# A head of column operations: part of one chunk's modulation on TensorE, its column operations moved, one weight load queued later

## The chip, the cores and the metric

The kernel runs on one core of a Trainium2 chip. The metric is device time in microseconds of one execution; the time shown for a kernel is the median of several executions. One further execution is recorded by the hardware profiler, and its trace is what is read below. TensorE (PE, with its weight loads PEld), VectorE (DVE), ScalarE (ACT), GpSimd (POOL) and SyncE (SP, which starts the DMAs) each run their own instructions in order and wait for one another by semaphores.

## The reference, cut to what matters

One layer of a decoder for 1024 tokens of width 1024: a mixing sub-layer (pooling and dilated window attention) and a gated MLP with a convolution, each between norms that are modulated by a conditioning vector. The change lies in the first lines, before the first projection:

```python
c_act = jax.nn.silu(c)
for l in range(DEPTH):
    mod = c_act @ w_ada[l] + b_ada[l]
    sh_m, sc_m, gt_m, sh_f, sc_f, gt_f = (t[:, None, :] for t in jnp.split(mod, N_MOD, axis=-1))
    h = rms_norm(x, g_pre_mix[l]) * (1.0 + sc_m) + sh_m
    y = mixing_sublayer(h, cos, sin, w_in[l], w_pool[l], b_pool[l], pool_scale[l], w_out[l])
    x = x + gt_m * rms_norm(y, g_post_mix[l])
    ...
```

`sh_m` and `sc_m`, 1024 numbers each, are what the touched code computes; `h @ w_in` inside `mixing_sublayer` is the projection that follows.

## The kernel before, in words

The head of the kernel works on six of the eight token tiles (`NS`) and goes through the width 1024 in eight chunks of 128 (`kc` from 0 to 7). For each chunk, `wa[kc]` holds the modulation weights: 128 partitions by eight pieces (`kb`) of 256 columns, 128 for the shift and 128 for the scale. The product with the conditioning vector goes in three steps. `mods_first` (L336 on ScalarE, L338 on VectorE) multiplies the pieces 0 and 1 by their column of `cact` into the two halves of `acc`. `mods(kc, 0)` adds the pieces 2 and 3, `mods(kc, 1)` the pieces 4 to 7 (six multiply-adds, L344) and then the two halves (L347), all on VectorE. `colsum` (L352) sums over the 128 partitions on TensorE: two matmuls of one column, with `acc` as the stationary operand, into the columns 256 and 257 of PSUM bank 7. `columns` (L355, L357, VectorE) makes of them one column of scale, `acol`, and one of shift, `bcol`.

Beside it, `turn` (L361) transposes the chunk of the six normalised token tiles into bank 6 and the first 256 columns of bank 7, and `h_chunk` lets ScalarE read them, apply `acol` and `bcol` and write `h` (L419) and its rounded copy `hh` (L417 for chunk 0, a copy at L124 for the others). `low` (L425, VectorE) makes the rest `hl`. `proj` then multiplies by the weights, which `piece` and `lower` (L391) have split into `wh` and `wl` in the same way: `hh` by `wh` and by `wl` (L410, L411), `hl` by `wh` (L407), into banks 0 to 5, one per token tile.

The order of all this is written out by hand for TensorE, ScalarE, VectorE and GpSimd. In the round of chunk `kc`, TensorE transposes chunk `kc`, sums its columns and projects chunk `kc - 1`, while VectorE adds up chunk `kc + 1`. Ahead of the rounds, three groups of `WARM` matmuls (L366, five each) on a constant stand between the norms of the token tiles. A weight chunk's buffer is one of three; chunk 4 takes that of chunk 1.

Behind the head, only TensorE's order is written by hand; a queue `Q` counts a slot for every group of three projection matmuls and runs tasks at their slot. The other engines' order is set by a scheduler. There, `unit_piece(1, j)` loads and splits a piece of the next unit's weights.

Of the kernel before, what the change touches and what calls it, by code (L numbers as in the profile page):

```python
# [12 lines left out]
AF = mybir.ActivationFunctionType  # L13
ALU = mybir.AluOpType

P = 128
# [63 lines left out]
WARM = (5, 5, 5)  # L80
NB = 2
# [24 lines left out]
def block_kernel(ctx: ExitStack, tc: tile.TileContext, x, pos, cols, rows, consts, w_ada_a, w_ada_b, w_in_u,  # L106
# [119 lines left out]
    NS = 6  # L226
# [65 lines left out]
    with tc.tile_pool(name="st", bufs=2) as st:  # L292
# [37 lines left out]
        def mods_first(kc, eng):  # L330
            if kc >= NK:
                return
            accs[kc] = st.tile([P, 2, 256], F32, name="acc", tag="acc", bufs=2)
            for i in range(2):
                if eng is nc.scalar:
                    nc.scalar.activation(accs[kc][:, i], wa[kc][:, i], AF.Copy, scale=cact[:, i:i + 1])  # L336
                else:
                    nc.vector.tensor_scalar_mul(accs[kc][:, i], wa[kc][:, i], cact[:, i:i + 1])  # L338

        def mods(kc, part):  # L340
            if kc >= NK:
                return
            for kb in range(4, 8) if part else (2, 3):
                nc.vector.scalar_tensor_tensor(accs[kc][:, kb % 2], wa[kc][:, kb], cact[:, kb:kb + 1],  # L344
                                               accs[kc][:, kb % 2], op0=ALU.mult, op1=ALU.add)
            if part:
                nc.vector.tensor_add(accs[kc][:, 0], accs[kc][:, 0], accs[kc][:, 1])  # L347

        def colsum(kc):
            for i in range(2):  # L350
                o, c = PS[:, 7, 256 + i:257 + i], slice(i * P, (i + 1) * P)
                nc.tensor.matmul(o, accs[kc][:, 0, c], ones[:, 0:1], start=True, stop=True)  # L352

        def columns(kc):
            nc.vector.tensor_scalar(acol[:, kc:kc + 1], PS[:, 7, 257:258], bsc1[:, kc:kc + 1], cl("g_pre_mix", kc),  # L355
# [3 lines left out]
        def turn(kc, ts_):  # L359
            for t in ts_:  # L360
                nc.tensor.transpose(PS[:, 6 + t // 4, (t % 4) * P:(t % 4 + 1) * P], xt[t][:, kc * P:(kc + 1) * P],  # L361
                                    ident)

        def warm(n):
            for _ in range(n):
                nc.tensor.matmul(bank(5, P), ones, ones, start=True, stop=True)  # L366
# [23 lines left out]
        def lower(j, wh, wl):  # L390
            nc.vector.tensor_tensor(wl, raws[j], wh.bitcast(F32), ALU.subtract)  # L391
# [35 lines left out]
        with tc.manual_schedule(engines={ET.PE, ET.Activation, ET.DVE, ET.Pool}):  # L427
            order = START.split()
            at = [0]

            def loads(n):
                for _ in range(n):
                    if at[0] < len(order):
                        load(order[at[0]][0], int(order[at[0]][1]))
                        at[0] += 1

            loads(FIRST_LOADS)
            nc.scalar.activation(cact, cl("c"), AF.Silu)
            angles()
            root(epst)  # L440
            mods_first(0, nc.vector)
            for part in range(2):
                mods(0, part)
            for t in range(0, NS, NB):
                norm_a(t, NB)
                if t == 0:
                    colsum(0)
                if t == NS - NB:
                    wh, wl = piece(0, False)
                norm_b(t, NB)  # L450
                turn(0, range(t, t + NB))
                warm(WARM[t // 2])
                if t == 0:
                    columns(0)
            h32 = h_chunk(0)
            mods_first(1, nc.vector)
            lower(0, wh, wl)
            mods(1, 0)
            mods(1, 1)
            low(0, h32)  # L460
            for kc in range(1, NK):
                loads(LOADS[kc])
                if kc == 1:
                    proj(0, 0, range(SPL))
                turn(kc, range(NS))
                if kc == 1:
                    proj(0, 0, range(SPL, NS))
                colsum(kc)
                mods_first(kc + 1, nc.scalar)
                mods(kc + 1, 0)  # L470
                columns(kc)
                h32 = h_chunk(kc)
                if kc == NRM:
                    norm_b(NS, 2)
                if kc in SQ_AT:
                    squares(NS + SQ_AT.index(kc))
                if kc == SQ_AT[1]:
                    roots[NS] = root(ssq[:, NS:NS + 2], 2)
                if kc > 1:
                    proj(kc - 1, 0)  # L480
                mods(kc + 1, 1)
                low(kc, h32)
                if kc in (1, 3, 5):
                    piece((kc + 1) // 2)
                proj(kc - 1, 1)
                if kc == 7:
                    turn_rest(0)
            loads(len(order))
            rest = h_rest(0)
            l_rest(0, rest)  # L490
            for t in range(NS):
                if t == RT:
                    turn_rest(1)
                proj(7, 0, (t,))
                proj(7, 1, (t,))
                if t < 2:
                    evac(un, t, t)
            piece(4)
            rope(un, 0)
            h32 = h_rest(1)  # L500
            l_rest(1, h32)
            piece(5)
            nc.vector.tensor_copy(cact2, cact)
# [96 lines left out]
    with tc.tile_pool(name="bp", bufs=1) as bp, tc.manual_schedule(engines={ET.PE}):  # L600
# [216 lines left out]
        for ui in range(5):  # L817
            if ui:
                un = Unit(ui, ws)
            un.V = new_v()  # L820
            if prev is not None:
                attend(prev, Q.slot + LAG_S)
            if ui == 1:
                catB = r2.tile([P, 2, 2, S], F32R, name="catB", tag="r2c")
                cat[2:4] = [(catB[:, 0, c], catB[:, 1, c]) for c in range(2)]
            if ui == 4:
                wps = [load_piece(w_in_p[1], 1024)]
            if ui:
                nxt = []
                for j, at_ in enumerate(PIECES):  # L830
                    Q.after(at_, lambda j=j, nxt=nxt, u=ui + 1: nxt.append(unit_piece(u, j)))
            else:
                nxt = more_w + [unit_piece(1, j) for j in (2, 3)]
            if MU <= ui <= MU + 2:
                for hf in range(2):
                    due = Q.slot + MLAG[hf]
                    later = lambda f, ahead=False, due=due: Q.at(due - MSPL * ahead, f)
                    if ui > MU:
                        mod_col(ui - MU, 7, hf, fin_shift if ui == MU + 1 else fin_scale, later)
                    elif hf:  # L840
                        Q.after(MLAG[0] + 1, lambda later=later: mod_row(0, 2, 6, gtg, 7, 1, later))
                    else:
                        mod_row(0, 2, 6, gtg, 7, 0, later)
            project(un, prev)
            ws, prev = nxt, un
# [671 lines left out]
```

## Time and profile before

| | us |
|---|---|
| median of 3 runs | 1058.23 (1057.42 to 1058.69) |
| the profiled execution's own time | 1057.68 |
| its span, first to last instruction | 1055.9 |
| TensorE busy | 1029.5 |
| VectorE busy | 850.7 |
| ScalarE busy | 487.9 |

The span is cut into groups of instructions with start, duration and what they waited for. A start in a row is in microseconds from the first instruction; the brackets at the end of a row of the timeline give the idle time ahead of it and what ended it.

### The profile page before, as it was taken

What the parts mean: (1) busy time and instruction counts of PE and PEld (TensorE: products, weight loads), DVE (VectorE), ACT (ScalarE), POOL (GpSimd) and SP (SyncE); (2) the same over time, 40 slices, a digit from 0 to 9 for tenths busy, and PEclk for the clock granted to TensorE, in tenths of its full rate; (3) what the DMA queues carried; (4) which work ended last, traced back from release to release, by engine and by line L of the source; (5) the groups of instructions that cost most, each with busy time, mean ns of one, the idle gap of its engine ahead of it and who ended that gap; (6) DMA issues with size and microseconds to landing.
All of it is one profiled execution on the core that took longest, in us unless ns stands there. A gap on an engine that the chain in (4) does not pass through costs nothing.

```text
span 1055.9 us, 15450 instructions
## 1 busy us (share of the span) xinstructions
PE 1029.5 (97%) x5174; PEld 871.8 (83%) x5174; DVE 850.7 (81%) x1839; ACT 487.9 (46%) x964; POOL 217.3 (21%) x132
## 2 busy tenths in 40 slices
PE   4999999999999999999999999999999999999997
PEld 4988989889888777878888888888888888888885
DVE  7975467885458768999999898998998798756997
ACT  6765343433354369733433333333334365544642
POOL 0000000000000000244334233333342415103560
PEclk9999999999999999999999999999999999999999
DMA  9552436362132173225334344444553889567553
GB/s 362 220 158 88 115 113 215 82 183 78 51 96 52 31 259 134 105 81 189 124 125 168 117 139 145 165 153 142 175 190 104 306 278 344 157 192 229 185 204 120
DMA packets 85148, 168.34 MB, mean 159 GB/s; under 512 B 9158, under 2 KB 25926, under 8 KB 81356
## 3 DMA queue, kind: packets, MB, share of 16 engines
q1 hardware_dynamic: 85068, 167.35, 47.7%
q8 instruction: 41, 0.67, 0.3%
q14 instruction: 39, 0.32, 0.1%
HBM read 134.47 MB, written 32.84 MB: 158 GB/s over the span
## 4 chain that ended last, share of the span: by engine, by line
PE 89%; DVE 5%; DMA 2%; ACT 2%; issue 1%; SPq 0%; DVEq 0%; ACTq 0%
PE PS L1092 36%; PE PS L1397 20%; PE PS L222 6%; PE PS L224 5%; PE PS L223 5%; PE PS L714 3%; PE PS L684 2%; PE PS L704 1%; DVE acc L344 1%; PE PS L596 1%; PE PS L598 1%; PE PS L597 1%; DMA wa<-in_w_ada_a_dram 1%; PE PS L622 1%; PE PS L781 1%
## 5 line engine op out<-in xcount | busy, mean ns | idle before, releaser
L1165 POOL TENSOR_TENSOR raws<-rw 128x512 f32<-128x512 f32 x28 | 45.6, 1627 | 510.8 <-PE PS L1092 442.9
L222 PE MATMUL PS<-wh,hh 128*128 128x384 f32 x336 | 124.4, 370 | 0.1
L224 PE MATMUL PS<-wh,hl 128*128 128x384 f32 x336 | 113.2, 337 | 0.0
L223 PE MATMUL PS<-wl,hh 128*128 128x384 f32 x336 | 112.9, 336 | 0.0
L1397 PE MATMUL PS<-tail 128*128 128x512 f32 x384 | 91.4, 389 | 0.0
L1092 PE MATMUL PS<-a,more 128*128 128x512 f32 x360 | 84.5, 389 | 0.0
L1397 PEld LDWEIGHTS PS<-tail 128*128 128x128 f32 x384 | 72.1, 188 | 15.0
L1092 PEld LDWEIGHTS PS<-a,more 128*128 128x128 f32 x360 | 67.6, 188 | 14.0
L124 ACT ACTIVATE more<-raws 128x512 fp32r<-128x512 f32 x67 | 41.5, 626 | 68.3 <-PE PS L1092 48.7
L222 PEld LDWEIGHTS PS<-wh,hh 128*128 128x128 f32 x336 | 63.5, 189 | 8.0 <-issue 4.5
L693 ACT ACTIVATE pm<-pm,nm 128x128 f32<-128x128 f32 (+1 forms) x96 | 42.4, 443 | 55.0 <-DVE nm L691 38.5
L687 DVE CUSTOM_DVE_ANT_0 pm<-PS,cst 128x128 f32<-128x128 f32 (+1 forms) x96 | 30.7, 348 | 44.3 <-PE PS L684 38.6
L223 PEld LDWEIGHTS PS<-wl,hh 128*128 128x128 f32 x336 | 63.5, 189 | 0.6 <-issue 0.5
L224 PEld LDWEIGHTS PS<-wh,hl 128*128 128x128 f32 x336 | 63.1, 188 | 0.0
L1092 PE MATMUL PS<-s,more 128*128 128x512 f32 x252 | 61.8, 393 | 0.2 <-DVE more L1161 0.2
L1161 DVE TENSOR_TENSOR more<-raws,more 128x512 fp32r<-128x512 f32 x63 | 58.6, 931 | 2.9 <-PE PS L1092 1.8
L1092 PE MATMUL PS<-b,more 128*128 128x512 f32 x252 | 60.5, 389 | 0.0
L1092 PEld LDWEIGHTS PS<-s,more 128*128 128x128 f32 x252 | 47.1, 188 | 11.6 <-issue 1.3
L1397 PE MATMUL PS<-more 128*128 128x512 f32 x240 | 56.5, 389 | 0.0
L1092 PEld LDWEIGHTS PS<-b,more 128*128 128x128 f32 x252 | 47.3, 188 | 9.8
L1203 ACT ACTIVATE cv<-cv 128x1024 f32<-128x1024 f32 x22 | 23.4, 1062 | 66.8 <-DVE cv L1201 66.8
L1397 PEld LDWEIGHTS PS<-more 128*128 128x128 f32 x240 | 45.0, 188 | 9.4
(345 smaller groups left out, 2540.4 us busy)
## 6 DMA issues: line engine op xcount, KB each, us to landing
rw<-in_w_up_dram SPq DMA_DIRECT2D x21, 1024.0 KB
gscr<-VV SPq DMA_DIRECT2D x66, 256.0 KB
mraw<-in_w_ada_b_dram SPq DMA_DIRECT2D x48, 256.0 KB
R<-in_w_down_dram SPq DMA_DIRECT2D x48, 256.0 KB
raw<-in_w_in_u_dram SPq DMA_DIRECT2D x24, 384.0 KB
wa<-in_w_ada_a_dram SPq DMA_DIRECT2D x8, 1024.0 KB
raws<-in_w_up_dram SPq DMA_DIRECT2D x28, 256.0 KB
R<-gscr SPq DMA_DIRECT2D x27, 256.0 KB
```

What stands on the lines that cost most here:

```text
L124: nc.scalar.activation(o, i, AF.Copy)
L222: nc.tensor.matmul(o, a, wh[:, c0:c0 + 384], start=k == 0, stop=False)
L223: nc.tensor.matmul(o, a, wl[:, c0:c0 + 384], start=False, stop=False)
L224: nc.tensor.matmul(o, b, wh[:, c0:c0 + 384], start=False, stop=k == 7)
L687: nc.vector.tensor_tensor_reduce(out=pm[:, h, 0:nk * P], in0=PS[:, 2 + h, 0:nk * P], in1=mask, op0=ALU.add, op1=ALU.max, scale=1.0, scalar ...
L693: nc.scalar.activation(pm[:, h, 0:nk * P], pm[:, h, 0:nk * P], AF.Exp, bias=nm[:, h:h + 1], scale=0.125, accum_out=U[:, h, HD + 1:HD + 2])
L714: nc.tensor.matmul(PS[:, 6, h * HD:(h + 1) * HD], pt[:, i * P:(i + 1) * P], un.V[:, k0 + kb, h * HD:(h + 1) * HD], start=kb == 0, stop=kb ...
L1092: nc.tensor.matmul(o, w_[:, k * P:(k + 1) * P], side(a, k)[low], start=i == 0, stop=i == 11)
L1161: nc.vector.tensor_tensor(wl, r, wh.bitcast(F32), ALU.subtract)
L1165: nc.gpsimd.tensor_tensor(t, a, b, ALU.add)
L1203: nc.scalar.activation(cv, cv, AF.Gelu_apprx_tanh)
L1397: nc.tensor.matmul(o, g[:, ts_], w, start=k == 0 and j == 0, stop=k == KD - 1 and j == 2)
```

## The change

Three things are edited. First, for chunk 1 alone, the weight pieces 0, 1 and 2 no longer go through VectorE: `direct(1)` multiplies them on TensorE, as six matmuls of one column with the weights as the stationary operand and a column of `cact` as the moving one, into the columns 256 and 257 of bank 7. It takes the place of the third group of warm-up matmuls. VectorE multiplies the pieces 4 and 3 and adds 5, 6 and 7; the two halves of `acc` are not added, and `colsum(1)`, now four matmuls, sums both on top of what `direct` left in PSUM. Second, orders change: `lower(0)` stands ahead of chunk 1's products, `colsum(1)` ahead of `turn(1)`, and `columns(1)` ahead of `mods(2, 0)`. Third, `unit_piece(1, 3)` is queued five slots later.

```diff
@@ mods_first, mods
+                kb = 4 - i if kc == 1 else i
...
-                    nc.vector.tensor_scalar_mul(accs[kc][:, i], wa[kc][:, i], cact[:, i:i + 1])
+                    nc.vector.tensor_scalar_mul(accs[kc][:, i], wa[kc][:, kb], cact[:, kb:kb + 1])
...
-            for kb in range(4, 8) if part else (2, 3):
+            for kb in range(5 if kc == 1 else 4, 8) if part else (2, 3):
...
-            if part:
+            if part and kc != 1:
                 nc.vector.tensor_add(accs[kc][:, 0], accs[kc][:, 0], accs[kc][:, 1])
+
+        def direct(kc):
+            for i in range(2):
+                o, c = PS[:, 7, 256 + i:257 + i], slice(i * P, (i + 1) * P)
+                for kb in range(3):
+                    nc.tensor.matmul(o, wa[kc][:, kb, c], cact[:, kb:kb + 1], start=i + kb == 0, stop=False)
@@ colsum
-                nc.tensor.matmul(o, accs[kc][:, 0, c], ones[:, 0:1], start=True, stop=True)
+                for j in range(2 if kc == 1 else 1):
+                    nc.tensor.matmul(o, accs[kc][:, j, c], ones[:, 0:1], start=kc != 1, stop=kc != 1 or i + j == 2)
@@ the written order
-                warm(WARM[t // 2])
+                if t == NS - NB:
+                    direct(1)
+                else:
+                    warm(WARM[t // 2])
...
             h32 = h_chunk(0)
+            lower(0, wh, wl)
             mods_first(1, nc.vector)
-            lower(0, wh, wl)
-            mods(1, 0)
             mods(1, 1)
             low(0, h32)
...
                     proj(0, 0, range(SPL))
+                    colsum(1)
                 turn(kc, range(NS))
                 if kc == 1:
                     proj(0, 0, range(SPL, NS))
-                colsum(kc)
+                else:
+                    colsum(kc)
                 mods_first(kc + 1, nc.scalar)
+                if kc == 1:
+                    columns(kc)
                 mods(kc + 1, 0)
-                columns(kc)
+                if kc > 1:
+                    columns(kc)
@@ the queue behind the head
-                nxt = more_w + [unit_piece(1, j) for j in (2, 3)]
+                nxt = more_w + [unit_piece(1, 2)]
+                Q.after(5, lambda nxt=nxt: nxt.append(unit_piece(1, 3)))
```

On TensorE, between the last transpositions of chunk 0 and the first projection, before (`xt` is a normalised token tile, `cst` holds the identity, `onesr` the constant of the warm-up):

```order
L361 MATMUL PS<-cst,xt_90 128x128 x2
L366 MATMUL PS<-onesr 128x128 x5
L410 MATMUL PS<-wh,hh 128x384
L411 MATMUL PS<-wl,hh 128x384
L410 MATMUL PS<-wh,hh 128x384
```

And further on there, from the third of the first projections to the sum of chunk 1's columns and the first matmuls on `hl`, before:

```order
L411 MATMUL PS<-wl,hh 128x384
L361 MATMUL PS<-cst,xt_88 128x128 x2
L361 MATMUL PS<-cst,xt_89 128x128 x2
L361 MATMUL PS<-cst,xt_90 128x128 x2
L410 MATMUL PS<-wh,hh 128x384
L411 MATMUL PS<-wl,hh 128x384
L410 MATMUL PS<-wh,hh 128x384
L411 MATMUL PS<-wl,hh 128x384
L410 MATMUL PS<-wh,hh 128x384
L411 MATMUL PS<-wl,hh 128x384
L352 MATMUL PS<-onesr,acc 128x1 x2
L407 MATMUL PS<-wh,hl 128x384 x6
```

The same stretch of TensorE in the changed kernel, from the last transpositions of chunk 0 to those of chunk 1:

```order
L369 MATMUL PS<-cst,xt_90 128x128 x2
L354 MATMUL PS<-cact,wa 128x1 x6
L418 MATMUL PS<-wh,hh 128x384
L419 MATMUL PS<-wl,hh 128x384
L418 MATMUL PS<-wh,hh 128x384
L419 MATMUL PS<-wl,hh 128x384
L418 MATMUL PS<-wh,hh 128x384
L419 MATMUL PS<-wl,hh 128x384
L360 MATMUL PS<-onesr,acc 128x1 x4
L369 MATMUL PS<-cst,xt_88 128x128 x2
L369 MATMUL PS<-cst,xt_89 128x128 x2
L369 MATMUL PS<-cst,xt_90 128x128 x2
```

The column sums stand ahead of the transpositions of chunk 1 and ahead of half of the first projections, and six matmuls of one column stand where the last five warm-up matmuls stood.

On VectorE, from the last norm to the start of chunk 2's sum, before (`acc` is the sum of products, `h_235` the `h` of chunk 0):

```order
L328 TENSOR_SCALAR xt_90<-xt_90,r_221 128x1024
L338 TENSOR_SCALAR acc<-wa,cact 128x256 x2
L391 TENSOR_TENSOR wl<-raw,wh 128x768
L344 SCALAR_TENSOR_TENSOR acc<-wa,cact,acc 128x256 x6
L347 TENSOR_TENSOR acc<-acc 128x256
L425 TENSOR_TENSOR hl<-h_235,hh 128x768
L344 SCALAR_TENSOR_TENSOR acc<-wa,cact,acc 128x256 x2
L355 TENSOR_SCALAR acol<-PS,bsc_96,col 128x1
L357 TENSOR_TENSOR bcol<-PS,col 128x1
L344 SCALAR_TENSOR_TENSOR acc<-wa,cact,acc 128x256 x4
L347 TENSOR_TENSOR acc<-acc 128x256
```

And in the changed kernel:

```order
L328 TENSOR_SCALAR xt_90<-xt_90,r_221 128x1024
L399 TENSOR_TENSOR wl<-raw,wh 128x768
L339 TENSOR_SCALAR acc<-wa,cact 128x256 x2
L345 SCALAR_TENSOR_TENSOR acc<-wa,cact,acc 128x256 x3
L433 TENSOR_TENSOR hl<-h_236,hh 128x768
L363 TENSOR_SCALAR acol<-PS,bsc_96,col 128x1
L365 TENSOR_TENSOR bcol<-PS,col 128x1
L345 SCALAR_TENSOR_TENSOR acc<-wa,cact,acc 128x256 x6
L348 TENSOR_TENSOR acc<-acc 128x256
```

Three multiply-adds and an add of chunk 1 are gone, the split of `wl` stands first, and the two column operations stand ahead of all six multiply-adds of chunk 2 instead of behind two of them. ScalarE's, GpSimd's and SyncE's instructions stand in the same order in both.

## Rows read from the trace of the kernel before

**Rows 1.** The page, busy time of TensorE, and the chain that ended last.

```profile
PE 1029.5 (97%) x5174; PEld 871.8 (83%) x5174; DVE 850.7 (81%) x1839; ACT 487.9 (46%) x964; POOL 217.3 (21%) x132
...
PE 89%; DVE 5%; DMA 2%; ACT 2%; issue 1%; SPq 0%; DVEq 0%; ACTq 0%
```

**Rows 2.** Stretches: length, busy PE, PEld, DVE, ACT, POOL; granted clock; DMA share, GB/s.

```profile
16.50:18.50 2.00, 2.00 (x11) 1.88 (x10) 1.45 (x6) 1.88 (x2) 0.00 (x0) 1.00 1.03 417
...
18.40:26.80 8.40, 7.25 (x49) 6.25 (x47) 8.27 (x21) 4.84 (x8) 0.00 (x0) 1.00 1.01 413
26.80:40.40 13.60, 13.44 (x84) 12.52 (x84) 13.50 (x32) 9.24 (x15) 0.00 (x0) 1.00 0.84 325
...
70.00:1050.00 980.00, 974.74 (x4849) 821.45 (x4847) 790.07 (x1665) 436.95 (x879) 217.13 (x128) 1.00 0.47 153
```

**Rows 3.** The chain of waits, 16 to 32 us: start, length, what.

```profile
19.94 2.38 DVE acc L344 x6
...
29.56 1.59 DVE acc L344 x4
```

**Rows 4.** Timeline of TensorE: start, length, engine, line, operation [idle before, releaser].

```profile
10.42 1.02 PE L352 MATMUL PS<-onesr,acc 128*128 128x1 f32 x4 [10.42 <-DVE acc L347]
...
16.50 2.08 PE L366 MATMUL PS<-onesr 128*128 128x128 f32 x10
18.52 0.45 PE L361 MATMUL PS<-cst,xt 128*128 128x128 f32 x2
18.80 1.28 PE L366 MATMUL PS<-onesr 128*128 128x128 f32 x10
20.05 0.45 PE L410 MATMUL PS<-wh,hh 128*128 128x384 f32 x1
...
21.23 0.81 PE L361 MATMUL PS<-cst,xt 128*128 128x128 f32 x6
...
22.94 0.50 PE L352 MATMUL PS<-onesr,acc 128*128 128x1 f32 x4
23.70 1.32 PE L407 MATMUL PS<-wh,hl 128*128 128x384 f32 x6 [0.26 <-DVE hl L425]
25.83 0.87 PE L361 MATMUL PS<-cst,xt 128*128 128x128 f32 x6 [0.81 <-ACT h L419]
26.78 0.61 PE L352 MATMUL PS<-onesr,acc 128*128 128x1 f32 x4
27.25 0.42 PE L410 MATMUL PS<-wh,hh 128*128 128x384 f32 x1
```

**Rows 5.** Timeline of VectorE.

```profile
18.46 0.61 DVE L338 TENSOR_SCALAR acc<-wa,cact 128x256 f32<-128x256 f32 x2 [0.39 <-DMA wa<-in_w_ada_a_dram]
18.99 0.95 DVE L391 TENSOR_TENSOR wl<-raw,wh 128x768 fp32r<-128x768 f32 x1
...
22.35 0.43 DVE L347 TENSOR_TENSOR acc<-acc 128x256 f32<-128x256 f32 x1
22.69 0.95 DVE L425 TENSOR_TENSOR hl<-h,hh 128x768 fp32r<-128x768 f32 x1
23.56 0.87 DVE L344 SCALAR_TENSOR_TENSOR acc<-wa,cact,acc 128x256 f32<-128x256 f32 x2
24.35 0.27 DVE L355 TENSOR_SCALAR acol<-PS,bsc,col 128x1 f32<-128x1 f32 x1
...
24.61 1.66 DVE L344 SCALAR_TENSOR_TENSOR acc<-wa,cact,acc 128x256 f32<-128x256 f32 x4
26.30 0.42 DVE L347 TENSOR_TENSOR acc<-acc 128x256 f32<-128x256 f32 x1
```

**Rows 6.** Timeline of ScalarE.

```profile
16.41 0.83 ACT L124 ACTIVATE wh<-raw 128x768 fp32r<-128x768 f32 x1
...
19.00 0.99 ACT L417 ACTIVATE hh<-PS,bcol,acol 128x768 fp32r<-128x768 f32 x1 [0.54 <-PE PS L361]
```

**Rows 7.** Timeline of TensorE, where the moved load's unit begins.

```profile
67.40 0.66 PE L622 MATMUL PS<-cst,qs 128*128 128x128 f32 x4 [1.15 <-DVE qs L289]
```

More of the change, by code (lines that the diff above doesn't have):

```diff
@@ L334, in mods_first @@
             for i in range(2):
+                kb = 4 - i if kc == 1 else i
                 if eng is nc.scalar:
-                    nc.scalar.activation(accs[kc][:, i], wa[kc][:, i], AF.Copy, scale=cact[:, i:i + 1])
+                    nc.scalar.activation(accs[kc][:, i], wa[kc][:, kb], AF.Copy, scale=cact[:, kb:kb + 1])
                 else:
-                    nc.vector.tensor_scalar_mul(accs[kc][:, i], wa[kc][:, i], cact[:, i:i + 1])
+                    nc.vector.tensor_scalar_mul(accs[kc][:, i], wa[kc][:, kb], cact[:, kb:kb + 1])
         def mods(kc, part):
```

## The prediction

> **What bounds the kernel now.** I read the page first. TensorE is busy for 97% of the span and carries 89% of the chain that ended last [rows 1]. So whatever moves the end must move TensorE's stream, and the table of stretches says where that stream is not yet full: from 70 to 1050 us it is busy for 974.74 of 980.00 us, while in the stretch that the change touches, 18.40 to 26.80 us, it lacks more than a microsecond and VectorE lacks almost nothing (8.27 of 8.40 us); from 26.80 to 40.40 VectorE is busy for 13.50 of 13.60 us [rows 2]. The chain of waits agrees: it runs along VectorE, through the modulation's multiply-adds (L344), at 19.94 as at 29.56, not along TensorE [rows 3]. Read rows 4 and 5 side by side with that in mind. For the second chunk VectorE does two products, six multiply-adds and an add before TensorE may sum the columns (L352 at 22.94); meanwhile TensorE waits 0.26 us for `hl` and 0.81 us for `h` [rows 4]. A loss in this head is handed on: each chunk's transpositions wait for the `h` of the chunk before, that for the column operations (L355, L357), and these stand in VectorE's full queue. Behind the head nothing starts by itself, so I take a shift of the head as a shift of the end, one for one.
>
> **The change, part by part.** (1) *VectorE is relieved.* Of the second chunk's nine operations, three multiply-adds and the add go: three of 0.40 us (six take 2.38 us) [rows 3] and 0.34 us (22.35 to 22.69) [rows 5], together 1.5 us. `lower(0)` now stands ahead of the products and fills the 0.39 us in which VectorE waited for the weights [rows 5]; its input is ready from 17.24 [rows 6]. VectorE's part of the second chunk is then over at 18.07 + 0.95 + 0.53 + 3 x 0.40 = 20.8 us instead of 22.78.
>
> (2) *TensorE gets six matmuls of one column in place of five warm-up matmuls.* A row of the trace counts each such matmul twice (two instructions of L352 are four records). Four records start 0.47 us apart from what follows and end 0.14 us later (26.78, 0.61 long, next at 27.25) [rows 4], so the twelve take 12 x 0.115 = 1.4 us from 18.80 and end at 20.3. The ten warm-up records lasted until 20.08 [rows 4]. On TensorE alone that is a loss of 0.2 us.
>
> (3) *But ScalarE now waits for them.* In the kernel before, `hh` of chunk 0 (L417) starts at 19.00, right behind the transpositions that end at 18.97 [rows 4, 6]. In the built program its wait is for TensorE's count 18, which the last transposition sets. In the changed program the transpositions no longer count by themselves; the wait is for count 24, which the last of the six one-column matmuls sets. Their sums lie in bank 7, of which ScalarE reads the first half. So `hh` starts at 20.3 + 0.03, not at 19.00, and the first projection (L410), which followed it by 1.05 us, at 21.4 instead of 20.05. Queued behind it on ScalarE are `h` of chunk 0 (to 22.2) and the products of chunk 2; VectorE's `low(0)` waits for that `h` and leaves VectorE idle from 20.8 to 22.2. [...]
>
> (4) *The columns of chunk 1.* From the first projection on: six matmuls (20.05 to 21.23, 1.18 us), the four column matmuls (eight records, 8 x 0.115 = 0.92 us), six transpositions (21.23, 0.81 us long) [rows 4]. The column operations wait for the end of all of it, since the program counts the column matmuls together with the transpositions behind them: 21.4 + 2.9 = 24.3 us at most, 24.1 with the shorter pace of 0.11 us. Before they started at 24.35 [rows 5]. So moving them ahead of chunk 2's multiply-adds gains 0 to 0.25 us for `h` of chunk 1, and not two microseconds. TensorE's waits for `hl` and `h` (1.07 us) go; the later start and the four added records have eaten them, for 1.35 + 0.46 us stand against 1.07 us: its next transpositions come at about 26.2 instead of 25.83.
>
> (5) *What is late next.* Chunk 2. At the end of the column operations VectorE had four multiply-adds and an add before it (24.61 to 26.72) [rows 5]; now all six stand behind them, since two were moved there: 2 x 0.4 = 0.79 us more (23.56 to 24.35) [rows 5]. VectorE idles for the same time ahead of the columns, from 23.1 to 24.2. Chunk 2's sum is thus ready at 26.72 + 0.79 - (0 to 0.25) = 27.26 to 27.51, and from there VectorE is as full as before, so `low`, `lower` and every column operation behind it come later by the same 0.5 to 0.8 us. TensorE's own delay of 0.4 us lies inside that. I take 0.6 us.
>
> (6) *The load moved by five groups.* `unit_piece(1, 3)` is queued five steps later in the text, but the built program has ScalarE's, GpSimd's and SyncE's instructions in the same order as before, loads included, and VectorE's and TensorE's too from the third chunk on, with the same waits. It costs nothing, because nothing moves. Had it moved, the price would be bounded by the wait of 1.15 us at 67.40 [rows 7], of either sign. Chunk 4's weights are asked for earlier, since the buffer is free at 20.8 and not at 22.3; nobody waits for them.
>
> **The sum.** 0 (load) + 0.6 us (head) on the profiled execution: 1055.9 us of span become 1056.5, its own time of 1057.68 becomes 1058.3. That execution lies 0.55 us below the median of the three runs, 1058.23, so the same shift on the median gives **1058.8 us**. Unknown in it: the pace of the one-column matmuls (0.11 to 0.118 us a record, 0.1 us in all), the columns' start (0.25 us), and some 0.6 us by which runs of the same kernel differ (1057.42 to 1058.69). A measurement of this kernel can tell about 0.2% from no change, 2.1 us; all of this is less.
>
> **Rivals.** *The wait costs nothing.* If `hh` could start at 19.00, the first projection would follow the one-column matmuls at 20.3, the columns come at 20.3 + 2.9 = 23.2 instead of 24.35, and chunk 2's sum at 26.72 - 1.15 + 0.79: 0.4 us earlier, 1057.8 us. For it speaks that the two use different columns of the bank; against it that the program makes the wait.
>
> *The load moves after all*, or shifts what ScalarE has ahead of the first `qs`: with the first rival at best 0.4 + 1.15 us faster, 1056.7 us. Not even that is 0.2%, and the order speaks against it.
>
> *TensorE's clock falls back, and the kernel is slower.* Warm-up matmuls of one size take 2.08 us for ten records from 16.50 and 1.28 us from 18.80 [rows 4], so the engine comes up to its full pace shortly before the replaced ones, though the column of the granted clock says 1.00 in all of it [rows 2]. At the lower pace four one-column records took 1.02 us (10.42) [rows 4]: (1.02 - 0.14) / 4 = 0.22 us each, so twelve take 2.6 us and end 1.2 us later. That alone makes 0.6 + 1.2 = 1.8 us, 1060.0 us, still not 0.2%. It decides from where the first projections also run at half pace: the 2.9 us to the columns become 5.8, the sum 4.7 us, 1062.9 us. For it: the replaced matmuls stream 128 columns and the new ones one, and TensorE then idles for about a microsecond (20.3 to 21.4). Against it: the rise lies before 18.80, where nothing on TensorE has changed, and gaps of 0.26 and 0.81 us within 2.5 us did not slow the matmuls that followed [rows 4]. [...]
>
> **How the numbers follow.** Forecast (the wait binds, +0.5 to +0.8 us): 0.70. No cost of the wait: 0.10. Half pace in the one-column matmuls alone, 1060.0: 0.07. Half pace in the projections too: 0.08. Load moved or something unseen that gains: 0.05. The first three are within 0.2%, and so is most of the last: same 0.88, slower 0.09, faster 0.03. The range takes in the first three with the runs' own scatter of 0.6 us on either side: from 1057.2 (1057.8 less 0.6) to 1060.6 (1060.0 and 0.6).
>
> **What would show it.** Right: `hh` of chunk 0 starts within 0.1 us of the last one-column matmul, at 20.2 to 20.4; VectorE idles from 20.8 to 22.2 and again before the columns at 24.1 to 24.4; chunk 2's add ends at 27.2 to 27.5; everything behind shifts by 0.5 to 0.8 us; the order around 67 us is as before. Wrong: `hh` at 19.0; or projections 0.35 us apart instead of 0.17; or a load or split that stands elsewhere at 60 to 75 us. Wrong in kind would be a head that loses and an end that does not, for then some later wait absorbs what I pass on one for one.

## Result: 3.2 us slower, over half of it by TensorE's clock

The changed kernel takes 1060.65 us (median of 10 runs, 1059.77 to 1061.71) against 1057.40 us for the kernel before in the same job: a ratio of 1.003, with an interval of 1.0021 to 1.0039. The forecast was 1058.8 us with a range up to 1060.6, and slower by over 0.2% had a chance of 0.09. The profiled execution of the changed kernel took 1060.76 us, 3.08 us more than that of before (1057.68). One execution of the runs below, the profiled one of e1_warm_kept, was disturbed (1286.55 us, mean granted clock 0.75) and is left out of every comparison.

Read the profile after in the order of the prediction. The page says the same as [rows 1]: TensorE is the bound, and it is busy for three microseconds more.

```profile
PE 1032.7 (98%) x5180; PEld 875.7 (83%) x5180; DVE 850.2 (80%) x1835; ACT 486.7 (46%) x964; POOL 218.0 (21%) x132
```

The table of stretches (length, busy PE, PEld, DVE, ACT, POOL, granted clock, DMA share, GB/s) answers to [rows 2], and there the surprise stands in the column behind POOL:

```profile
18.40:26.80 8.40, 7.32 (x40) 7.23 (x39) 4.11 (x11) 3.20 (x5) 0.00 (x0) 0.70 1.01 414
26.80:40.40 13.60, 13.60 (x86) 13.49 (x86) 13.50 (x32) 8.85 (x14) 0.00 (x0) 0.93 0.65 254
70.00:1050.00 980.00, 975.38 (x4854) 822.14 (x4853) 790.27 (x1667) 437.30 (x882) 217.84 (x128) 1.00 0.46 153
```

The granted clock of the first stretch is 0.70, where it was 1.00 before. Cut into single microseconds, it is 1.00 up to 21 us, 0.50 from 22 to 28 us and back at 1.00 from 29 us:

```profile
20.00:21.00 1.00, 0.04 (x1) 0.00 (x0) 0.62 (x2) 0.92 (x2) 0.00 (x0) 1.00 1.01 418
21.00:22.00 1.00, 0.88 (x4) 0.88 (x5) 0.01 (x1) 1.00 (x3) 0.00 (x0) 0.88 1.05 418
22.00:23.00 1.00, 1.00 (x6) 1.00 (x5) 0.94 (x1) 0.74 (x2) 0.00 (x0) 0.50 0.96 401
...
28.00:29.00 1.00, 1.00 (x6) 1.00 (x5) 0.96 (x4) 1.00 (x3) 0.00 (x0) 0.70 0.00 0
29.00:30.00 1.00, 1.00 (x12) 0.97 (x10) 1.00 (x3) 0.67 (x2) 0.00 (x0) 1.00 0.00 0
```

The timeline of TensorE in the changed kernel (start, length, line, operation, idle time ahead in brackets) shows what that does, beside [rows 4]:

```profile
18.64 1.40 PE L354 MATMUL PS<-cact,wa 128*128 128x1 f32 x12
21.12 0.45 PE L418 MATMUL PS<-wh,hh 128*128 128x384 f32 x1 [1.08 <-ACT hh L425]
...
21.77 0.51 PE L419 MATMUL PS<-wl,hh 128*128 128x384 f32 x1
22.07 0.52 PE L418 MATMUL PS<-wh,hh 128*128 128x384 f32 x1
22.39 0.52 PE L419 MATMUL PS<-wl,hh 128*128 128x384 f32 x1
22.71 1.70 PE L360 MATMUL PS<-onesr,acc 128*128 128x1 f32 x8
24.27 1.52 PE L369 MATMUL PS<-cst,xt 128*128 128x128 f32 x6
...
27.51 1.71 PE L415 MATMUL PS<-wh,hl 128*128 128x384 f32 x6
29.06 0.82 PE L369 MATMUL PS<-cst,xt 128*128 128x128 f32 x6
```

The six one-column matmuls (twelve records, as the trace counts each twice) end at 20.04 for the forecast 20.3, and TensorE then idles for 1.08 us, as forecast. But from 21.77 on the projections stand 0.32 us apart instead of 0.17, six transpositions last 1.52 us instead of 0.81, and the transpositions of chunk 2 come at 29.06 instead of 25.83. TensorE waits for nothing there; it is slow. ScalarE and VectorE wait for it. ScalarE:

```profile
20.08 0.99 ACT L425 ACTIVATE hh<-PS,bcol,acol 128x768 fp32r<-128x768 f32 x1 [1.77 <-PE PS L354]
```

and VectorE:

```profile
21.98 0.96 DVE L433 TENSOR_TENSOR hl<-h,hh 128x768 fp32r<-128x768 f32 x1 [1.36 <-ACT h L427]
25.83 0.28 DVE L363 TENSOR_SCALAR acol<-PS,bsc,col 128x1 f32<-128x1 f32 x1 [2.89 <-PE PS L369]
...
28.58 0.42 DVE L348 TENSOR_TENSOR acc<-acc 128x256 f32<-128x256 f32 x1
```

ScalarE starts `hh` behind the last one-column matmul, 0.04 us after it. The column operations, forecast for 24.1 to 24.4 us, come at 25.83, and chunk 2's sum ends at 29.0.

Some waits further on give a part back. A shift is taken here between two rows of the same TensorE instructions in the two traces: 3.23 us at the transpositions of chunk 2 (29.06 for 25.83). It is 2.13 us at the group of twelve matmuls that begins at 1021.62 in the kernel before, and from there to the end it grows once more, by 0.90 us. TensorE of the kernel before there:

```profile
1021.62 2.88 PE L1397 MATMUL PS<-tail,more 128*128 128x512 f32 x12
...
1036.58 0.84 PE L1397 MATMUL PS<-more 128*128 128x512 f32 x3
```

and of the changed kernel:

```profile
1023.75 2.88 PE L1413 MATMUL PS<-tail,more 128*128 128x512 f32 x12
...
1039.03 0.74 PE L1413 MATMUL PS<-tail 128*128 128x512 f32 x2 [0.24 <-DVE tail L171]
1039.61 0.87 PE L1413 MATMUL PS<-more 128*128 128x512 f32 x3
```

Here TensorE waits for VectorE's last `tail`, as it does not at this place in the kernel before. So the loss has two parts: 2.13 us from the head and 0.90 us in the last 100 us. Their sum, 3.03 us, is the 3.08 us between the two executions.

### The profile page after: what moved, and what is told of

Read it like the earlier page. It is cut to its first block, busy times and chain, and to the rows that moved or that the text cites. A ratio compares the mean times of both kernels' runs of the same rounds, so it can differ in the third digit from the quotient of the medians.

```text
span 1059.0 us, 15459 instructions
## 1 busy us (share of the span) xinstructions
PE 1032.7 (98%) x5180; PEld 875.7 (83%) x5180; DVE 850.2 (80%) x1835; ACT 486.7 (46%) x964; POOL 218.0 (21%) x132
## 4 chain that ended last, share of the span: by engine, by line
PE 88%; DVE 6%; ACT 3%; DMA 2%; issue 1%; SPq 0%; DVEq 0%; ACTq 0%
PE PS L1108 36%; PE PS L1413 18%; PE PS L222 6%; PE PS L224 5%; PE PS L223 5%; PE PS L729 3%; PE PS L699 2%; PE PS L719 1%; PE PS L611 1%; PE PS L613 1%; PE PS L612 1%; DVE acc L345 1%; PE PS L637 1%; PE PS L796 1%; PE PS L798 1%
```

## The experiments

Three questions: what lowers the clock; what the wait, the columns and the order are worth while it stays up; where the 0.90 us come from. Times are against the kernel before in the same job (medians 1057.40 for the change, then 1057.35, 1057.66 and 1057.53 us). "Head" is TensorE's shift against the trace of before at 1021.62, "end" that at 1036.58; the end agrees with the difference of the two profiled executions' own times within 0.1 us. Between 60 us and 1021.62 the shift moves by up to 0.6 us where nothing was edited (e14_padded_only has -0.47 at 60 us), so a few tenths in "head" say little.

The traces are one execution each, but the mean granted clock over the whole span is on record for every execution. In 76 executions of the kernel before it is 0.998 or 0.999. In the traces with a fall in the head it is 0.993 to 0.997, in those without 0.998 or 0.999. The column "low" counts the executions with 0.997 or less; one with 0.998 may still hide a short fall.

| run | median us | ratio, interval | clock in the head (trace) | low | head | end |
|---|---|---|---|---|---|---|
| the change | 1060.65 | 1.003, 1.0021 to 1.0039 | 0.50, 22 to 28 us | 9 of 10 | +2.13 | +3.03 |
| e10_after_again | 1061.33, one run | | 0.50, 21 to 30 us | 1 of 1 | +3.17 | +3.63 |
| e4_columns_unused | 1057.69 | 1.0002, 0.9993 to 1.001 | 1.00 | 3 of 11 | +0.21 | +0.21 |
| e5_wait_only | 1058.01 | 1.0005, 0.9996 to 1.0014 | 1.00 | 0 of 11 | +0.24 | +0.24 |
| e8_columns_and_gap | 1059.68 | 1.002, 1.0011 to 1.003 | 1.00 | 5 of 10 | +0.35 | +0.35 |
| e15_columns_and_gap_again | 1059.79, one run | | 0.50, 23 to 25 us | 1 of 1 | +2.07 | +2.09 |
| e1_warm_kept | 1058.90 | 1.0016, 1.0007 to 1.0025 | | 1 of 10 | | |
| e11_warm_again | 1058.51, one run | | 1.00 | 0 of 1 | +0.34 | +0.77 |
| e2_own_banks | 1057.22 | 0.9996, 0.9987 to 1.0005 | 1.00 | 4 of 11 | -1.45 | -0.47 |
| e13_own_banks_again | 1057.61 | 1.0001, 0.9992 to 1.001 | 0.50, 22 to 25 us | 4 of 10 | -1.55 | -0.41 |
| e12_own_banks_padded | 1057.47 | 0.9999, 0.9991 to 1.0008 | 1.00 | 5 of 11 | -1.40 | -0.29 |
| e9_delay_only | 1060.91 | 1.003, 1.0019 to 1.0042 | 1.00 | 0 of 6 | +2.83 | +2.83 |
| e14_padded_only | 1057.93 | 1.0004, 0.9995 to 1.0013 | 1.00 | 0 of 10 | +0.11 | +0.11 |

e11_warm_again is the same kernel as e1_warm_kept, and the trace below is its own.

### Is it the missing dense matmuls, or the idle time?

Into the kernel before, once the thin matmuls in place of the dense ones, written into a bank that ScalarE does not read, and once the dense ones written into bank 7, so that ScalarE waits for them:

```diff
-                warm(WARM[t // 2])
+                if t == NS - NB:
+                    for i in range(2):
+                        for kb in range(3):
+                            nc.tensor.matmul(PS[:, 5, 256 + i:257 + i], wa[1][:, kb, i * P:(i + 1) * P],
+                                             cact[:, kb:kb + 1], start=True, stop=True)
+                else:
+                    warm(WARM[t // 2])
```

> The kernel before with its third group of warm-up matmuls replaced by the same six one-column matmuls, into bank 5, where nobody reads them; VectorE still does the whole modulation, and ScalarE does not wait for them. Theory (it takes the one-column matmuls and the idling behind them together): no gap on TensorE, the clock stays at 1.00, time within 0.2 us of the kernel before, 1057.4 us. Rival (replacing the dense warm-up matmuls is enough): the clock falls to 0.50 for some 7 us from about 21.8 us, and since VectorE bounds the head, the time rises by 1 to 2.5 us.

```diff
-        def warm(n):
+        def warm(n, o):
...
-                nc.tensor.matmul(bank(5, P), ones, ones, start=True, stop=True)
+                nc.tensor.matmul(o, ones, ones, start=True, stop=True)
...
-                warm(WARM[t // 2])
+                warm(WARM[t // 2], PS[:, 7, 384:512] if t == NS - NB else bank(5, P))
```

> The kernel before with its third group of warm-up matmuls writing into the unused end of bank 7 instead of bank 5, so that ScalarE's read of banks 6 and 7 waits for them; nothing else differs. It has the wait and the idling of about 1.1 us without the one-column matmuls. Theory (wait and clock are separate costs, and the idling alone does not lower the clock): hh of chunk 0 starts near 20.1 us, the first projection near 21.2, and as VectorE's sum of chunk 1 ends at 22.8 anyway, the head ends 0.1 to 0.4 us later: 1057.6 us, clock 1.00. Rival (a gap of a microsecond after the first warm-up is enough to lower the clock): granted clock 0.50 for some 7 us, 1059 us or more.

The clock stays at 1.00 in both traces. In e5_wait_only TensorE idles just as long as in the changed kernel, and the matmuls behind keep their pace, as these two rows of its timeline show:

```profile
20.94 0.44 PE L410 MATMUL PS<-wh,hh 128*128 128x384 f32 x1 [1.08 <-ACT hh L417]
21.22 0.34 PE L411 MATMUL PS<-wl,hh 128*128 128x384 f32 x1
```

Its price by itself: nothing at 25.83, where the chunk's transpositions start as before, since the wait there is 0.37 us instead of 0.81. The shift is still 0.00 at 60 us; the 0.24 us at the end come later and are no more than what shifts move by without an edit.

The means of all executions tell the two apart. With the idle time alone none of eleven is low. With the thin matmuls alone three of eleven are, at 1057.94 to 1058.15 us, where the other eight have a median of about 1057.4. So this gap alone did not bring the clock down, and the thin matmuls alone did in some executions, at a price of about 0.5 us in this head.

### Both together, and nothing else of the change

The edit is that of e4_columns_unused with another place for the results:

```diff
...
+                            nc.tensor.matmul(PS[:, 7, 384 + i:385 + i], wa[1][:, kb, i * P:(i + 1) * P],
+                                             cact[:, kb:kb + 1], start=True, stop=True)
...
```

> The kernel before, with the third warm-up group replaced by six one-column matmuls whose results nobody reads, written into bank 7: so the one-column matmuls and the wait of ScalarE's hh on them stand there together, and nothing else of the change. Neither alone lowered the clock. Theory (TensorE's clock falls where the thin matmuls and the idle time behind them come together): TensorE idle 1.0 to 1.2 us before the first projection, granted clock near 0.5 for some 7 us from 21.8 us on, projections 0.35 us apart, the end 1.5 to 2.3 us later, 1058.9 to 1059.7 us. Rival (the fall needs the moved columns of chunk 1 or the freed VectorE as well): the clock stays at 1.00, the projections 0.17 us apart, at most 1058.0 us.

> The kernel before with six unread one-column matmuls into bank 7 in place of the third warm-up group, for a second trace. The first trace had the clock at 1.00 throughout and was the fastest execution (1058.12 us); the other nine took 1059.6 to 1060.6 us. If those are executions in which the clock fell: an execution over 1059.5 us shows a granted clock near 0.5 for some 4 to 8 us between 20 and 30 us and projections 0.32 us apart there, and one under 1058.5 us does not.

The median is +2.02 us, with executions of two kinds: one of 1058.12 us, which is the traced one, and nine of 1059.56 to 1060.57. The traced one kept its clock. The second trace is of an execution of 1059.79 us, and there the clock falls. Its stretches, columns as above:

```profile
22.00:23.00 1.00, 1.00 (x7) 0.97 (x7) 1.00 (x2) 1.00 (x3) 0.00 (x0) 0.77 1.03 410
23.00:24.00 1.00, 1.00 (x6) 1.00 (x5) 1.00 (x3) 0.01 (x1) 0.00 (x0) 0.50 0.93 373
24.00:25.00 1.00, 1.00 (x5) 1.00 (x4) 0.06 (x1) 0.00 (x0) 0.00 (x0) 0.50 1.08 432
25.00:26.00 1.00, 1.00 (x6) 1.00 (x5) 0.00 (x0) 0.00 (x0) 0.00 (x0) 0.53 0.99 399
26.00:27.00 1.00, 1.00 (x8) 1.00 (x9) 0.63 (x3) 0.19 (x1) 0.00 (x0) 1.00 0.73 303
```

Same program, +0.35 us with the clock up and +2.07 us with it down: 1.7 us for something over three microseconds at half pace. The columns' order and VectorE's relief aren't in this kernel, so the loss of the head does not need them. Of the nine late executions five have a mean clock of 0.996 or 0.997, as this second one (0.996). The other four (1059.56, 1060.12, 1060.30 and 1060.57 us) have 0.998, as the kernel before has, and what made them late no trace shows. A first rise that comes late would not lower the mean, since the column says 1.00 ahead of the rise too (ten warm-up records take 2.08 us at 1.00, [rows 2, 4]); that is a possibility and not shown.

### The changed kernel with its dense matmuls back

```diff
                 if t == NS - NB:
                     direct(1)
-                else:
-                    warm(WARM[t // 2])
+                warm(WARM[t // 2])
```

> The changed kernel with the third group of five warm-up matmuls put back, behind the six one-column matmuls; nothing else differs. Theory: the changed kernel loses most of its 3.2 us because TensorE's granted clock falls to 0.50 from 21.8 to 28.7 us, after 1.4 us of one-column matmuls and 1.08 us of idling; with the warm-up matmuls in that gap the clock stays at 1.00, the projections stand 0.17 us apart, and only ScalarE's wait is left: 0.5 to 0.8 us over the kernel before, about 1058.1 us, mean clock as before. Rival (the wait for the bank and the later chain are the loss, and the clock only accompanies it): 1060.3 to 1061 us as the changed kernel, whatever the clock does.

> The change with the third warm-up group kept behind the one-column matmuls, for a trace. Its time is 1.5 us over the kernel before. Theory (head as forecast, tail as in the change): clock 1.00 in the head, a shift of 0.5 to 0.8 us by 70 us and some 0.9 us more after 955 us. Rival (the clock still falls for a while): granted clock under 0.9 somewhere in 21 to 29 us and a shift of 1.3 to 1.6 us by 70 us, the same at the end.

The ten dense records fit into the time in which TensorE would idle, and the clock stays; the loss goes from 3.25 us to 1.55 us. TensorE and VectorE of e11_warm_again, timelines:

```profile
18.39 1.40 PE L354 MATMUL PS<-cact,wa 128*128 128x1 f32 x12
19.65 1.36 PE L374 MATMUL PS<-onesr 128*128 128x128 f32 x10
20.87 0.45 PE L418 MATMUL PS<-wh,hh 128*128 128x384 f32 x1
...
26.95 0.61 PE L360 MATMUL PS<-onesr,acc 128*128 128x1 f32 x4 [0.50 <-DVE acc L348]
```

```profile
23.73 0.28 DVE L363 TENSOR_SCALAR acol<-PS,bsc,col 128x1 f32<-128x1 f32 x1 [1.03 <-PE PS L369]
...
26.48 0.42 DVE L348 TENSOR_TENSOR acc<-acc 128x256 f32<-128x256 f32 x1
```

This is the head as it was forecast. This execution started 0.37 us earlier than that of before (first matmul at 10.05, not 10.42); with that added the columns come at 24.1 and chunk 2's sum ends at 27.27, and TensorE waits for that sum, which it did not before. The head loses 0.34 us, or 0.71 with the earlier start taken off, where 0.6 was forecast. The run as a whole is +1.55 us, its traced execution +0.83: what the other 0.7 us are, no trace shows. A fall of the clock is not in sight for them: one of e1's ten executions is low (1059.65 us), and the slowest, 1061.10 us, has a mean clock of 0.999.

### The sums in banks of their own

```diff
-                o, c = PS[:, 7, 256 + i:257 + i], slice(i * P, (i + 1) * P)
+                o, c = PS[:, 4 + i, 256:257], slice(i * P, (i + 1) * P)
...
                 turn(kc, range(NS))
                 if kc == 1:
+                    columns(kc)
                     proj(0, 0, range(SPL, NS))
...
```

> The changed kernel with chunk 1's column sums in banks 4 and 5 instead of bank 7, so that ScalarE's first read of banks 6 and 7 need not wait for the one-column matmuls; the column operations of chunk 1 stand ahead of the last three first projections, which reuse these banks. Theory: hh of chunk 0 starts at 18.9 us and not at 20.1, the first projection follows the one-column matmuls without a gap at about 20.1, the clock stays at 1.00, and chunk 2's sum is ready 0.8 to 1.2 us earlier than in the kernel before: about 1056.4 us. Rival (one-column matmuls make the clock fall, with or without a gap behind them): the clock falls to 0.50 near 21.8 us all the same and the time stays over 1058.5 us.

In the trace of e2_own_banks the first projection follows the last one-column matmul without a gap, and the column operations wait for the column sums alone:

```profile
18.41 1.40 PE L354 MATMUL PS<-cact,wa 128*128 128x1 f32 x12
19.67 0.43 PE L419 MATMUL PS<-wh,hh 128*128 128x384 f32 x1
```

```profile
21.80 0.28 DVE L364 TENSOR_SCALAR acol<-PS,bsc,col 128x1 f32<-128x1 f32 x1 [0.32 <-PE PS L360]
```

They come at 21.80 instead of 24.35 [rows 5], and the head is 1.45 us shorter. Of that 0.98 us are lost at the end. The version gains no time that can be measured: the other two runs of this head are at 0.9999 and 1.0001.

> The change with its sums in banks of their own once more, beside the padded one, for a second trace: 1057.0 to 1057.4 us, 1.4 to 1.5 us early up to 955 us. If the loss of 1.0 us in the last 100 us belongs to this program it comes again, within 0.3 us; if it is an execution's accident, 0 to 1 us.

The second trace shows the clock at 0.50 from 22 to 25 us **without** idle time ahead of it, and still 1.55 us gained at 1021.62: the matmul that starts at 24.64 is 1.87 us late against the kernel before, and by 51 us all of that is made up. So the fall does not need the gap. Of the 32 executions of the three runs with this head 13 are low; the two lowest, at 0.995, are the slowest of their runs (1059.63 and 1059.11 us), so that a longer fall seems to cost something here too, while this short one cost nothing in a head with time to spare on TensorE.

### The last 100 us

From 24.61 us of the trace of before to its end, the two traces show the same instructions in the same order on TensorE, VectorE, ScalarE and GpSimd. Yet every trace of a kernel with the change's VectorE work loses 0.4 to 1.1 us there. Is it the late arrival?

```diff
                 proj(kc - 1, 1)
+                if kc == 5:
+                    for _ in range(19):
+                        nc.tensor.matmul(PS[:, 7, 384:512], ones, ones, start=True, stop=True)
```

> The kernel before, with 19 dense warm-up matmuls of 0.115 us (2.2 us) on TensorE behind the second pass of chunk 4's projections, near 50 us: a pure delay of the size that the change has by 70 us, and nothing else. Theory 1 (a delay of the head costs one for one): 2.1 to 2.3 us, 1059.5 to 1059.7 us, and the shift against the kernel before stays the same from 70 us to the end. Theory 2 (the last 100 us are sensitive to when things come, and the late head itself cost the 0.9 us more there): 1060.3 to 1060.7 us, with a shift that grows after 955 us.

Nineteen instructions are 38 records, so the delay was twice as long as meant:

```profile
43.85 4.46 PE L488 MATMUL PS<-onesr 128*128 128x128 f32 x38
```

1.5 us of it are made up by 70 us; the other 2.8 us come out at the end undiminished and not enlarged, +2.83. In this trace lateness alone is passed on one for one. (It is of the fastest of six executions; the median, +3.25 us, is 0.4 us later, and no trace shows why.) Is it then the place of VectorE's instructions in their stream? The change has four fewer.

```diff
     nc.vector.memset(epst, EPS)
+    nc.vector.memset(epst, EPS)
+    nc.vector.memset(epst, EPS)
+    nc.vector.memset(epst, EPS)
+    nc.vector.memset(epst, EPS)
```

> The change with its sums in banks of their own (as in the run named own_banks), and four one-element-wide memsets more on VectorE at the start of the program, where it waits for its first load, so that every later VectorE instruction has the number that it has in the kernel before. The change has four VectorE instructions fewer than the kernel before, and in all four traces of kernels with that difference the last 100 us lost 0.4 to 1.0 us, in none of the five without it. Theory 1 (the place of VectorE's instructions in the stream decides that loss): the head's 1.4 to 1.5 us stay to the end, 1056.0 to 1056.4 us. Theory 2 (the loss comes from when VectorE and GpSimd happen to meet): 1056.8 to 1057.4 us, as without the memsets.

> The kernel before with four small memsets more on VectorE at the start of the program, where it waits for its first load; nothing else. Theory 1 (the place of VectorE's instructions in the stream decides the loss of the last 100 us): 0.4 to 1.0 us later, 1057.8 to 1058.5 us, with a constant shift up to 955 us. Theory 2 (it does not): within 0.2 us of the kernel before.

It is not: with the numbers aligned the loss is 1.11 us, and with four more in the kernel before it is 0. What decides is how far VectorE lags behind TensorE. The end of its last `tail` in the kernel before, in the changed kernel, and in e12_own_banks_padded:

```profile
1034.70 0.68 DVE L171 TENSOR_TENSOR tail<-raws,tail 128x512 fp32r<-128x512 f32 x1
```

```profile
1038.30 0.67 DVE L171 TENSOR_TENSOR tail<-raws,tail 128x512 fp32r<-128x512 f32 x1
```

```profile
1035.00 0.67 DVE L175 TENSOR_TENSOR tail<-raws,tail 128x512 fp32r<-128x512 f32 x1
```

VectorE's shift at this row less TensorE's at 1021.62 is 3.60 - 2.13 = 1.47 us in the change and 0.30 + 1.40 = 1.70 in e12_own_banks_padded; the losses are 0.90 and 1.11 us, 0.57 and 0.59 less. In the four others that lose (e2, e10, e11, e13; lags of 1.00 to 1.72) the difference is 0.57 to 0.58 as well, and in the six runs with a lag under that (-0.73 in e9_delay_only to 0.48 in e15_columns_and_gap_again) nothing or 0.03 is lost. So VectorE has 0.58 us to spare at that place, and what it lags beyond that TensorE waits. Why the kernels with the change's code lag by 1.00 us and more in all six traces, and the others by 0.48 at most, stays open. The lag builds up from about 955 to 1005 us, a stretch in which some operations of VectorE last until one of GpSimd ends (1.2 to 1.3 us for 0.15 in the kernel before, below); that these make up the lag is a guess that no run shows.

### The changed kernel again

> The changed kernel as it is, for a second trace. If the clock's fall belongs to the kernel: granted clock near 0.50 from 21.8 to 28.7 us once more and a shift of 2.1 to 2.3 us against the kernel before by 70 us. If the 0.9 us more after 955 us belongs to it: a shift of 2.9 to 3.2 us at the last projection's end; if that was one execution's accident: 2.1 to 2.4 us there.

The fall comes again, earlier and for longer (0.71 from 20 to 21 us, 0.50 to 30 us), and so the head loses 3.17 us instead of 2.13. The end adds 0.46 us, so of the two parts the first is the larger in both traces. Of the ten executions of the result nine are low. The tenth has a mean clock of 0.998 and took 1060.24 us, no less than the others, so for that one the clock is not shown to be the cause.

## Why the prediction was wrong

**What bounds the head.** Right for the kernel before. In the changed kernel the head is bound by TensorE at half pace, and what VectorE saved is idle time: 2.89 us ahead of the columns.

**(1) VectorE's relief and (2) the matmuls' price.** Right within 0.3 us: ended at 20.04 against 20.3, because they started 0.16 us earlier (18.64 for 18.80) and a record took a little under the 0.115 us of the sum (twelve take 1.40 us with the end of the last, which the sum put 0.14 us behind them).

**(3) ScalarE's wait.** Right in kind and size: `hh` 0.04 us behind the last matmul, first projection at 21.12 for 21.4, an idle gap of 1.08 us. What the wait costs by itself in the changed kernel no run shows (in the kernel before it cost nothing by 60 us, e5_wait_only); with the banks apart and the columns freed from the transpositions, both at once, e2_own_banks has a head 0.34 + 1.45 = 1.8 us shorter than e11_warm_again. The first rival's 0.4 us faster was sized too low, as it kept the columns behind the transpositions.

**(4) and (5) Columns and chunk 2.** Right where the clock stays: 24.1 and 27.27 us in e11_warm_again for 24.1 to 24.3 and 27.26 to 27.51. The cost was 0.34 to 0.71 us for 0.5 to 0.8. One sum inside is not right: 1.35 + 0.46 - 1.07 = 0.74 us puts TensorE's next transpositions at 26.6 and not at 26.2; they came at 26.0 (25.64 and 0.37), and nothing hung on it. In the changed kernel itself all of this is overrun by the clock.

**(6) The load.** Right: nothing moves.

**The step that failed** is the argument against the third rival. It had the right cause, a fall of the clock (0.50 from 22 to 28 us) with half pace in the projections (0.32 us apart for 0.17), and 1062.9 us as its price. It was given 0.08, because the rise of the pace lies ahead of 18.80, and because idle times of 0.26 and 0.81 us in [rows 4] had not slowed what followed. Both rows are true and neither is a test. The rise is where one execution had it: in the traces of e4_columns_unused and e15_columns_and_gap_again the twelve one-column records took 1.59 and 1.60 us and not 1.40, so that TensorE was not yet at full pace when they began. And no more than four records of one column stood ahead of those idle times, with dense matmuls around them.

What the runs showed in its place: thin matmuls without dense ones behind them bring the clock down in some executions (3 of 11 in e4_columns_unused), with a gap behind them in more (9 of 10 in the change, at least 5 of 10 in e8_columns_and_gap), and the same gap behind dense matmuls in none of 11 (e5_wait_only). The price was put too high: 2.1 to 3.2 us in the head and 3.0 to 3.6 at the end instead of 4.7. The one-column matmuls themselves ran at full pace (1.40 us where this rival had 2.6), the clock comes back by 29 to 31 us, and waits further on absorb a part.

**The smaller one** is "one for one". It holds for lateness (2.83 us in, 2.83 us out), but the shift of the end is that of TensorE plus whatever VectorE lags over 0.58 us at 1036 us. That added 0.90 and 0.46 us in the change, and it took 1.0 to 1.1 us of the 1.4 to 1.55 us that banks of their own had gained.

**Range and chances.** The median is 0.05 us above the upper end, and that it is so near is luck: the forecast was counted from 1058.23 us, and the kernel before took 1057.40 over ten executions. Against its own base the forecast's upper end is +2.4 us, and the change measured +3.25. The range left out the case that came true, and "slower by over 0.2%", which came, had 0.09.

## What to carry to other kernels

Five dense matmuls whose results nobody reads had a price here when they went: thin ones in their place and a gap behind them made nine of ten executions low, with the dense ones put back one of ten was. Before replacing such matmuls with thin ones, look at what stands behind, and either fill the idle time that a new wait opens with dense ones, as there, or take the wait away. The second, here by banks of their own, did not keep the clock up (13 of 32 low), but left TensorE time to make up for it (1.87 us late in e13_own_banks_again, made up by 51 us). Judge a possible fall of the clock by the rows around the new instructions and by many executions, not by one trace and not by gaps elsewhere that had dense work ahead of them. And when a head gets shorter or longer, look for the engine with the least to spare at the far end before passing the shift on.

## What the runs showed of the hardware

**The clock falls late and not always.** By the mean granted clock of each microsecond it fell at about 21.8 us in the change and 22.5 us in e15_columns_and_gap_again, where TensorE was busy again, and at 20.4 us, in the gap, in e10_after_again. With thin matmuls and no dense ones behind them it fell in four traces of eight (three of four with the gap, one of four without); with dense ones behind them, or without thin ones, in none of five, that of before among them. Over all executions on record 32 of 65 are low with thin matmuls and no dense ones behind them, and one of 38 in the other runs; of the kernel before none of 76. It came back at 25 to 31 us. Two traces of one program differ already ahead of the thin matmuls: the same ten warm-up records took 1.28 us in e8_columns_and_gap, which kept its clock, and 2.34 us in e15_columns_and_gap_again, which lost it:

```profile
16.37 1.28 PE L366 MATMUL PS<-onesr 128*128 128x128 f32 x10
```

```profile
16.14 2.34 PE L366 MATMUL PS<-onesr 128*128 128x128 f32 x10
```

How early TensorE came up does not decide by itself: they took 2.34 us in e4_columns_unused too, which kept its clock, and 1.55 us in e10_after_again, which lost it.

**Some small operations of VectorE end together with one of GpSimd.** In the kernel before, three VectorE operations on 128x1 elements, which take 0.15 us elsewhere, last 1.2 to 1.3 us. VectorE, and below it GpSimd, timelines:

```profile
992.89 1.26 DVE L162 SCALAR_TENSOR_TENSOR v<-v,r 128x1 f32<-128x1 f32 x1
...
994.20 1.21 DVE L163 SCALAR_TENSOR_TENSOR r<-v,r 128x1 f32<-128x1 f32 x1
...
1000.24 1.28 DVE L161 TENSOR_TENSOR v<-v,r 128x1 f32<-128x1 f32 x1
```

```profile
992.46 1.68 POOL L1322 TENSOR_TENSOR R<-R,R 128x512 f32<-128x512 f32 x1 [2.22 <-DMA R<-in_w_down_dram]
994.09 1.30 POOL L1322 TENSOR_TENSOR gm<-gm,R 128x512 f32<-128x512 f32 x1
999.70 1.80 POOL L1322 TENSOR_TENSOR raws<-raws,R 128x512 f32<-128x512 f32 x1 [4.31 <-DMA raws<-in_w_down_dram]
```

Each began inside a GpSimd operation and ended within 0.02 us of it (994.15 and 994.14, 995.41 and 995.39, 1001.52 and 1001.50). That VectorE waits there for GpSimd is a reading of these three ends, and what would make it wait no run shows. Which operations meet differs between traces: in that stretch of the changed kernel one 128x1 operation is drawn out (1.14 us, to 997.84, where GpSimd's ends at 997.82) and not three.
